# Attention values as float32 products on two column halves of TensorE, without a split of the exponentials

## The chip, the core and the metric

The kernel runs on one core of a Trainium2 chip, in one launch. The metric is the device time of that launch in microseconds (us). The engines of the core work side by side from their own queues, in the order in which the program lists their instructions: TensorE (PE in the profile; PEld is its loading of stationary operands), VectorE (DVE), ScalarE (ACT), GpSimd (POOL) and SyncE (SP), which issues most of the DMA transfers.

## The reference, cut to what matters

One layer of a diffusion backbone works on 128 context tokens and 1024 latent tokens: a modulated norm, one input projection, two branches (multi-head attention, and an mLSTM in two directions), a merge, an output projection and a feed-forward part. The change touches the attention alone. It has 8 heads, 96 numbers for a query or key and 64 for a value:

```
s = einsum('bqhd,bkhd->bhqk', qn_b, k_nope) + einsum('bqhr,bkr->bhqk', qp_b, k_pe)
p = softmax(s.astype(float32) * MLA_SCALE, axis=-1)
out = einsum('bhqk,bkhv->bqhv', p, v)
```

A context token attends to the 128 context keys. A latent token attends to 1152 keys: 1024 latent ones and 128 from a cache. All data are float32.

## The kernel before, in words

Most products in this kernel are made with a faster number format of TensorE, float32r, that keeps fewer bits. So each operand is first split in two parts: a leading part (`hi`, line 69, a copy on ACT) and the rest (`lo`, line 75, a subtraction on DVE). `mm3` (lines 95 to 100) then adds three products of such parts. Plain float32 products are used too: in the mLSTM (lines 1079 to 1084) and for sums over partitions (line 1449, for one).

The attention (`attention`, line 1183) goes through 40 units of work. Eight heads have five units each: four with 256 latent queries and nine blocks of 128 keys, and one with the 128 context queries and one block. A latent unit has five steps, of two key blocks each and one in the last. `scores` makes the scores of a step transposed, keys on the partitions, in the PSUM tile `st`; ACT takes their exponentials into `p` (line 1403). Then `p` is split: `ph` on ACT, `pl` on DVE (steps 0, 1 and 3) or on POOL (steps 2 and 4, line 1407). POOL adds up the exponentials in `es` (lines 1418 to 1422). Two steps later `values` multiplies `ph` and `pl` of each block by `v`, a stationary operand of 128 columns: 64 with the leading parts of the values, 64 with the rest (lines 1437 and 1438). All products of a unit add up in one PSUM tile `pv`.

`output` ends a unit in three pieces: the sums of the exponentials for each query, by float32 products with a column of ones (line 1449); their reciprocals, split into `rh` and `rl` and written on the diagonals of `dr` by ACT (line 1459); two products of 64 columns that spread them over 64 partitions (line 1462). Then the two halves of `pv` are added (line 1466), multiplied by the reciprocals (line 1467), split and stored to `d_att`.

Three things run beside it. `maxima` takes, one unit ahead, the greatest score of each query: products `mx` (line 1372), a DVE reduction of each (line 1374, `sm`), and a product that turns the result into a row (line 1382). `o_mlstm` multiplies the mLSTM output `hm` by its projection (tile `mm`, 384 columns). `head_load` and `head_split` fetch and split the next head's queries, keys and values, one piece a step. The instructions are recorded in one order and then placed on each engine by a scheduler that simulates a timeline; the engines follow that order and wait with semaphores.

Of the kernel before, what the change touches and what calls it, by code (L numbers as in the profile page):

```python
# [10 lines left out]
F32 = mybir.dt.float32  # L11
R32 = mybir.dt.float32r
# [7 lines left out]
P = 128  # L20
# [17 lines left out]
AV = 64  # L38
# [14 lines left out]
def f32v(ap):  # L53
    return ap.bitcast(F32)


class K:
# [25 lines left out]
    def load_w(self, src, kt, w, bufs=None):  # L83
        """Stream one weight block [P, kt, w] from DRAM and split it exactly."""
# [27 lines left out]
    def rsqrt(self, ssq, width, n, pool):  # L112
        """1/sqrt(ssq/n + eps) on the vector engine: exponent estimate and three Newton steps."""
# [12 lines left out]
    def row_rstd(self, rbc, acc, n, pool, pp, tag, chunks=CHUNKS, more=None):  # L126
        """rbc[:, t] = 1/sqrt(sum_p (acc[p, t] + more[p, t])/n + eps) on every partition."""
# [30 lines left out]
    def modulate(self, raw, t, sc, sh, k):  # L158
        """raw = t * sc + sh with the context's and the sample's own columns."""
# [4 lines left out]
    # ------------------------------------------------------------------  # L164
# [74 lines left out]
    def tick(self, n=1):  # L239
        """Emit n pieces of the work that runs beside the products."""  # L240
# [7 lines left out]
    def store(self, *args):  # L248
        """A store that is issued later, so that the loads behind it need not wait for its data."""
        self.stores.append(args)  # L250
# [8 lines left out]
    def rows(self, rbc, acc, n, pool, pp, tag):  # L259
        """rbc[:, t] = 1/sqrt(sum_p acc[p, t]/n + eps) on every partition."""  # L260
# [28 lines left out]
    def inputs(self):  # L289
        """Everything that reads the modulated input (all of w_in), the mLSTM and the attention's projections."""  # L290
# [38 lines left out]
    def start(self, vp):  # L329
        """Norm and modulation of the input, and the mLSTM's values."""  # L330
# [44 lines left out]
        def row(f):  # L375
            """Shift (f even) or scale of block 6 + f // 2 of the features, as rows against the broadcast condition."""
# [166 lines left out]
    def t_ops(self, X, xp):  # L543
        """The four sums on the moving side."""
# [29 lines left out]
    def z_lat(self, x):  # L574
        """Latents and their norms, and the tile with gates and rotary key."""
# [40 lines left out]
    def z_qk(self, h, x):  # L616
        """q and k of one mLSTM head, S^T and k^T."""
# [29 lines left out]
    def z_big(self, p, x):  # L647
        """sigmoid(zmo) * g_mlstm for tiles 0-7, the sigmoids of the branch gates after them."""
# [17 lines left out]
    def background(self):  # L666
        """Columns of the modulation that are used after the mixer, as rows against the broadcast condition."""
# [41 lines left out]
    def krope(self):  # L709
        """Rotary keys, 288 tokens to a row."""  # L710
# [16 lines left out]
    def gates(self):  # L727
        """Every per-token scalar of the two scans; row 64 d + 9 h + c holds chunk c of head h in direction d,
        whose scans run along the row, backwards for d = 1."""
# [66 lines left out]
        # N = -M, A = log of the denominator's floor  # L796
# [24 lines left out]
    def lat_kv(self):  # L821
        """The key and value latent, back from DRAM and split."""
# [19 lines left out]
    def stage(self):  # L842
        """Half a slot for a projected block."""
# [11 lines left out]
    def proj(self):  # L855
        """Keys, values and queries of the attention from the latents."""
# [94 lines left out]
    def fill(self, n=1):  # L951
        """Emit n column chunks of the attention's projections."""
# [5 lines left out]
    # ------------------------------------------------------------------  # L958
# [80 lines left out]
    def mfront(self, d, c, carried, second, S, E, Q, W):  # L1039
        """Operands of one chunk of one direction, four heads."""  # L1040
# [20 lines left out]
    def mback(self, d, c, carried, second, A, Q, K, C, mp, pp, side, load):  # L1061
        """Products, state update and output of the chunk."""
# [46 lines left out]
    def mpost(self, c, out, ssq, sgs, mp, pp):  # L1109
        """Norm, output gate and transposition of a finished chunk."""  # L1110
# [22 lines left out]
    # ------------------------------------------------------------------  # L1133
    def operands(self, pool):
        """Queries, keys and values of one head in two parts; row 96 adds -max of a query to its scores."""
        q = pool.tile([QK + 1, 2, T], R32, name=self.nm("q"))
        k = pool.tile([QK + 1, 2, NK], R32, name=self.nm("k"))
        v = pool.tile([P, NCH + 1, P], R32, name=self.nm("v"))
# [4 lines left out]
    def head_load(self, h, pool=None):  # L1143
        """Queries, keys (context, latent, cache) and values of one head, as column blocks."""
        G = self.nc.sync
        v = self.wp.tile([P, NCH + 1, AV], F32, name=self.nm("rv"), tag="wr", bufs=self.wb[0])
# [18 lines left out]
        G.dma_start(v, self.d_vo[h])  # L1165
        return q, k, v

    def head_split(self, h, raw):
        q, k, v = self.sets[h % 2]
        rq, rk, rv = raw  # L1170
# [5 lines left out]
        self.hi(v[:, :, 0:AV], rv)  # L1176
        self.lo(v[:, :, AV:], rv, v[:, :, 0:AV])
        yield 1

    SLOTS = 5  # L1180
    LAG = 2

    def attention(self):
# [6 lines left out]
        with tc.tile_pool(name="at", bufs=1, reuse_waits="tile") as ap:  # L1190
            self.ap, self.pp = ap, pp
            first = lambda shape, tag, bufs, dt=R32: ap.tile(shape, dt, name=self.nm(tag), tag=tag, bufs=bufs)
            for tag in ("ph", "pl"):
                first([P, 2, 256], tag, 4)
            first([P, 2, 256], "es", 2, F32)
            first([P, 2, 2, P], "dr", 1)
# [3 lines left out]
            self.onr = ap.tile([P, AV], R32, name="onr")  # L1200
            self.hi(self.onr, self.ones[:, 0:AV])
# [74 lines left out]
    def first(self):  # L1276
        """The first three products of two tiles of features, which don't wait for the last heads."""
# [15 lines left out]
    def early(self):  # L1293
        """The outputs of the first heads, in place of the operands of the last even one."""
# [9 lines left out]
    def fload(self, f, g, t):  # L1304
        """The gate of the attention's branch and the other branch."""
# [746 lines left out]
```

## Time and profile before

| | |
|---|---|
| time, median of 3 runs (lowest, highest) | 2248.58 us (2246.25, 2249.5) |
| span of the profiled execution, first to last instruction | 2242.8 us |
| the profiled execution's own time around the span | not given apart from the span; the median lies 5.8 us above it |
| PE busy, share of the span | 2083.1 us, 93% |
| DVE | 1659.5 us, 74% |
| ACT | 1068.0 us, 48% |
| POOL | 1127.2 us, 50% |
| granted TensorE clock, mean | 0.966 of full speed |
| attention, from its first product `mx` (848 us) to the last of `pv` (1263 us) | 415 us |

Busy time of PE counts an instruction until its modelled end, and a product begins before the one ahead of it has ended, so that a busy PE may still be waiting between starts. How much of the stage is really streamed is seen from the starts of successive products, or from their number and the distance between them.

### The profile page before, as it was taken

The numbers are of one execution on the slowest core, as the hardware profiler recorded it, in microseconds if no ns is written. First come the engines' busy times: TensorE is split into PE (matmuls) and PEld (weight loads), VectorE is DVE, ScalarE is ACT, GpSimd is POOL, SyncE is SP. The second block draws the span as 40 slices with busy tenths as digits, with TensorE's granted clock in tenths as the row PEclk, the third lists the DMA queues.
The fourth block names the chain that finished last, engine by engine and source line by source line (L and its number), as shares of the span: only waits on it lengthen the run. The fifth ranks groups of instructions, "written<-read, shape, count | busy, mean of one in ns | idle before, by whom it ended". The sixth has DMA issues, their size and how long they took to land.

```text
span 2242.8 us, 40186 instructions
## 1 busy us (share of the span) xinstructions
PE 2083.1 (93%) x14713; PEld 1998.2 (89%) x14713; DVE 1659.5 (74%) x2998; ACT 1068.0 (48%) x2225; POOL 1127.2 (50%) x850
## 2 busy tenths in 40 slices
PE   6799999999989987999999999879999999989898
PEld 2799998999978776998998999879999999989897
DVE  6725745988845879998987666899755565799895
ACT  4322333445445556777776435444322222356464
POOL 3612122667624415877877543677867634431411
PEclk8899999999999998999999999999999999999899
DMA  7121244555479775322224575223555522557664
GB/s 286 63 93 59 90 142 124 164 174 183 152 241 330 238 230 175 90 74 65 84 66 102 170 224 157 86 83 122 186 177 183 175 89 80 161 173 248 206 201 138
DMA packets 234532, 340.97 MB, mean 152 GB/s; under 512 B 18110, under 2 KB 170398, under 8 KB 233310
## 3 DMA queue, kind: packets, MB, share of 16 engines
q1 hardware_dynamic: 225790, 328.73, 46.0%
q0 software_dynamic: 4848, 6.06, 1.1%
q10 hardware_dynamic: 3696, 3.61, 0.5%
q8 instruction: 116, 1.90, 0.4%
q14 instruction: 82, 0.67, 0.1%
HBM read 250.55 MB, written 87.80 MB: 151 GB/s over the span
## 4 chain that ended last, share of the span: by engine, by line
PE 42%; DVE 16%; DMA 7%; POOL 6%; issue 6%; ACT 2%; SPq 1%; DVEq 0%; POOLq 0%; ACTq 0%
PE mm L98 10%; PE mm L100 10%; PE mm L99 10%; DVE wo L75 4%; DMA pr<-w_fo 3%; DVE sm L1374 2%; DVE pl L75 1%; PE st L98 1%; PE pv L1437 1%; PE pv L1438 1%; PE st L100 1%; PE st L99 1%; PE mx L1372 1%; DMA N<-d_nm 1%; PE p L1079 1%
## 5 line engine op out<-in xcount | busy, mean ns | idle before, releaser
L100 PE MATMUL mm<-th,wo 128*128 128x288 f32 x1840 | 546.8, 298 | 14.0 <-DVE wo L75 13.7
L98 PE MATMUL mm<-th,wo 128*128 128x288 f32 x1840 | 547.6, 298 | 2.7 <-DVE zo L1658 1.1
L99 PE MATMUL mm<-tl,wo 128*128 128x288 f32 x1840 | 546.2, 297 | 0.0
L100 PEld LDWEIGHTS mm<-th,wo 128*128 128x128 f32 x1840 | 348.9, 190 | 18.2 <-DVE wo L75 17.6
L75 DVE TENSOR_TENSOR wo<-wr,wo 128x512 fp32r<-128x512 f32 (+1 forms) x317 | 314.6, 1008 | 59.4 <-ACT wo L69 54.4
L98 PEld LDWEIGHTS mm<-th,wo 128*128 128x128 f32 x1840 | 348.2, 189 | 4.5 <-issue 1.6
L99 PEld LDWEIGHTS mm<-tl,wo 128*128 128x128 f32 x1840 | 348.3, 189 | 0.1
L69 ACT ACTIVATE wo<-wr 128x512 fp32r<-128x512 f32 (+1 forms) x317 | 187.5, 607 | 147.9 <-PE mm L100 69.5
L69 ACT ACTIVATE wo<-ws 128x512 fp32r<-128x512 f32 x188 | 116.7, 627 | 271.7 <-PE mm L100 160.5
L75 DVE TENSOR_TENSOR wo<-ws,wo 128x512 fp32r<-128x512 f32 x188 | 186.7, 996 | 62.1 <-ACT wo L69 61.9
L100 PE MATMUL mm<-xh,wo 128*128 128x288 f32 x616 | 184.7, 301 | 10.3 <-DVE wo L75 10.3
L1642 POOL TENSOR_TENSOR ws<-wr,ws 128x512 f32<-128x512 f32 x47 | 62.3, 1326 | 243.5 <-DVE wo L75 238.2
L99 PE MATMUL mm<-xl,wo 128*128 128x288 f32 x616 | 184.7, 300 | 0.0
L98 PE MATMUL mm<-xh,wo 128*128 128x288 f32 x616 | 184.2, 299 | 0.5 <-ACT wo L69 0.5
L1420 POOL TENSOR_TENSOR es<-es,p 128x512 f32<-128x512 f32 (+1 forms) x96 | 129.4, 1348 | 34.8 <-ACT p L1403 19.9
L98 PE MATMUL mm<-B,wo 128*128 128x288 f32 x456 | 134.8, 296 | 2.6 <-DVE zo L1658 1.7
L100 PE MATMUL mm<-B,wo 128*128 128x288 f32 x456 | 134.8, 296 | 0.0
L99 PE MATMUL mm<-B,wo 128*128 128x288 f32 x456 | 134.8, 296 | 0.0
L701 POOL TENSOR_TENSOR wm<-wm,sr 128x512 f32<-128x512 f32 x64 | 100.1, 1567 | 65.2 <-DVE mj L700 49.2
L100 PEld LDWEIGHTS mm<-xh,wo 128*128 128x128 f32 x616 | 118.1, 192 | 12.7 <-DVE wo L75 12.5
L98 PEld LDWEIGHTS mm<-xh,wo 128*128 128x128 f32 x616 | 118.2, 192 | 0.7 <-ACT wo L69 0.7
L99 PEld LDWEIGHTS mm<-xl,wo 128*128 128x128 f32 x616 | 118.4, 192 | 0.0
(443 smaller groups left out, 6076.6 us busy)
## 6 DMA issues: line engine op xcount, KB each, us to landing
wr<-w_ff SPq DMA_DIRECT2D x56, 512.0 KB
wm<-wm SPq DMA_DIRECT2D x32, 512.0 KB
wr<-d_w SPq DMA_DIRECT2D x32, 512.0 KB
d_z<-zo SPq DMA_DIRECT2D x48, 288.0 KB
d_g<-uu SPq DMA_DIRECT2D x44, 288.0 KB
wr<-w_big SPq DMA_DIRECT2D x24, 512.0 KB
wr<-w_fo SPq DMA_DIRECT2D x24, 512.0 KB
pr<-w_fo SPq DMA_DIRECT2D x40, 256.0 KB
```

The source lines that it names most:

```text
L69: i = self.nc.scalar.activation(out, in_, AF.Copy)
L75: return self.nc.vector.tensor_sub(out, in_, f32v(hi)).ins
L98: mm(out, lhs[0], rhs[0], start=first, stop=False)
L99: mm(out, lhs[0], rhs[1], start=False, stop=False)
L100: self.pe = mm(out, lhs[1], rhs[0], start=False, stop=last).ins
L701: nc.gpsimd.tensor_tensor(w[:, n], w[:, n], sr[:, 1], op=ALU.mult)
L1079: self.pe = mm(p1, A[:, h], V[:, h], start=True, stop=not carried).ins
L1372: nc.tensor.matmul(s[:, :kc], q[0:QK, 0, q0 + t * P:q0 + (t + 1) * P], k[0:QK, 0, k0 + j * kc:k0 + (j + 1) * kc], start=True, stop=True)
L1374: nc.vector.tensor_reduce(sm[:, 3 * t + j:3 * t + j + 1], s[:, :kc], axis=AX.X, op=ALU.max, negate=True)
L1420: G.tensor_tensor(U["sum"][:, :m], U["sum"][:, :m], p[:, :m], op=ALU.add)
L1437: nc.tensor.matmul(pv[:, :n], v[:, i], ph[:, e, :n], start=c + e == 0, stop=False)
L1642: G.tensor_tensor(s4, a12, s2, op=ALU.subtract)
```

## The change

The exponentials are not split any more, and neither are the values. `p` has six buffers of its own and goes into the products as float32, with `v` as 64 float32 columns. The two key blocks of a step are multiplied one after the other in the program, the first on columns 0 to 63 of TensorE (partitions 0 to 63 of `pv`), the second on columns 64 to 127. The last block, which has no partner, is cut in two halves of the queries that go the same way. The sums of the exponentials are made by one float32 product with a stationary operand of ones, 64 columns wide, which leaves the sum of each query on all 64 partitions; DVE then takes the reciprocal of a tile of 64x256 and multiplies by it. The values of the next head are fetched straight into their place, at the beginning of `head_split` in place of the end of `head_load`. Comments are taken out as well, which moves line numbers.

```diff
 def operands(self, pool):
-        v = pool.tile([P, NCH + 1, P], R32, name=self.nm("v"))
+        v = pool.tile([P, NCH + 1, AV], F32, name=self.nm("v"))
...
 def head_load(self, h, pool=None):
-        v = self.wp.tile([P, NCH + 1, AV], F32, name=self.nm("rv"), tag="wr", bufs=self.wb[0])
...
-        G.dma_start(v, self.d_vo[h])
-        return q, k, v
+        return q, k
 def head_split(self, h, raw):
         q, k, v = self.sets[h % 2]
-        rq, rk, rv = raw
+        rq, rk = raw
+        self.nc.sync.dma_start(v, self.d_vo[h])
...
-        self.hi(v[:, :, 0:AV], rv)
-        self.lo(v[:, :, AV:], rv, v[:, :, 0:AV])
-        yield 1
...
+    PBUF = 6
...
 def scores(self, U, c):
-        p = self.wp.tile([P, 2, 256], F32, name=self.nm("p"), tag="ws", bufs=3)
+        p = ap.tile([P, 2, 256], F32, name=self.nm("p"), tag="p", bufs=self.PBUF)
         self.ia = nc.scalar.activation(p[:, :m, :n], st[:, :m, :n], AF.Exp).ins
-        ph, pl = (ap.tile([P, 2, 256], R32, name=self.nm(x), tag=x, bufs=4) for x in ("ph", "pl"))
-        self.hi(ph[:, :m, :n], p[:, :m, :n])
-        if c in (2, 4):
-            nc.gpsimd.tensor_tensor(pl[:, :m, :n], p[:, :m, :n], f32v(ph[:, :m, :n]), op=ALU.subtract)
-        else:
-            self.iv = self.lo(pl[:, :m, :n], p[:, :m, :n], ph[:, :m, :n])
-        U["P"][c] = ph, pl
+        U["P"][c] = p
...
 def values(self, U, c):
-        ph, pl = U["P"].pop(c)
-        for e, i in enumerate(kb[2 * c:2 * c + 2]):
-            nc.tensor.matmul(pv[:, :n], v[:, i], ph[:, e, :n], start=c + e == 0, stop=False)
-            self.pe = nc.tensor.matmul(pv[:, :n], v[:, i], pl[:, e, :n], start=False, stop=i == kb[-1]).ins
+        p = U["P"].pop(c)
+        blocks = kb[2 * c:2 * c + 2]
+        if len(blocks) == 2:
+            parts = [(i, e, 0, n) for e, i in enumerate(blocks)]
+        else:
+            parts = [(blocks[0], 0, t * n // 2, n // 2) for t in range(2)]
+        for g, (i, e, q0, w) in enumerate(parts):
+            self.pe = nc.tensor.matmul(pv[g * AV:(g + 1) * AV, q0:q0 + w], v[:, i], p[:, e, q0:q0 + w], start=c == 0,
+                                       stop=c == U["nc"] - 1, skip_group_check=True).ins
...
 def output(self, U):
-        for t in range(nt):
-            nc.tensor.matmul(pv[:, 256 + t:257 + t], U["sum"][:, 0, t * P:(t + 1) * P], self.ones[:, 0:1], start=True, stop=True)
-        rd = ap.tile([P, 2], F32, name=self.nm("rd"), tag="rd", bufs=2)
-        nc.vector.reciprocal(rd[:, :nt], pv[:, 256:256 + nt])
...
-        for t in range(nt):
-            for e, x in enumerate((f32v(rh), rl)):
-                nc.scalar.activation(dg[:, e, t], self.ident, AF.Copy, scale=x[:, t:t + 1])
+        nc.tensor.matmul(pv[0:AV, 256:256 + n], self.ones[:, 0:AV], U["sum"][:, 0, :n], start=True, stop=True, skip_group_check=True)
         yield 1
-        for e in range(2):
-            nc.tensor.matmul(pv[0:AV, 256:256 + n], self.onr[:, 0:AV], dg[:, e, :nt].rearrange("p t q -> p (t q)"),
-                             start=e == 0, stop=e == 1)
...
+        rd = ap.tile([AV, 256], F32, name=self.nm("rd"), tag="rd", bufs=2)
+        nc.vector.reciprocal(rd[:, :n], pv[0:AV, 256:256 + n])
+        nc.vector.tensor_mul(t2[:, :n], t2[:, :n], rd[:, :n])
```

On TensorE before, in the second head: the end of a unit (`onr` by `dr`) and the first step of the next, whose two key blocks take four products.

```order
L1462 MATMUL pv_10018<-dr_10101,onr 64x128 x2
L1382 MATMUL mx_10265<-selr,mr_10154 1x256
L1437 MATMUL pv_10064<-ph_9973,v_9240 128x256
L1438 MATMUL pv_10064<-pl_9974,v_9240 128x256
L1437 MATMUL pv_10064<-ph_9973,v_9240 128x256
L1438 MATMUL pv_10064<-pl_9974,v_9240 128x256
L98 MATMUL mm_9987<-hm_9373,wh_9757 128x384
```

On TensorE now, in the same head: two steps of a unit. `x2` stands for two products of one form, here those of the two key blocks.

```order
L1429 MATMUL pv_9876<-p_9835,v_9235 64x256 x2
L1365 MATMUL mx_9863<-k_9234,q_9233 128x384
L98 MATMUL st_9903<-q_9233,k_9234 128x256
L99 MATMUL st_9903<-q_9233,k_9234 128x256
L100 MATMUL st_9903<-q_9233,k_9234 128x256
L1429 MATMUL pv_9876<-p_9857,v_9235 64x256 x2
L98 MATMUL mm_9819<-hm_9397,wh_9641 128x384
L99 MATMUL mm_9819<-hm_9397,wh_9641 128x384
```

The four products of a step have become two of half the width, one behind the other, with products of full width on both sides.

On DVE before, between two reductions of the maxima: the split of exponentials, and reciprocals with their split.

```order
L75 TENSOR_TENSOR pl_9806<-p_9803,ph_9805 128x512
L1467 TENSOR_TENSOR av_9727<-av_9727,pv_9522 64x256
L1377 TENSOR_REDUCE mr_9912<-sm_9911 128x1
L1451 RECIPROCAL rd_9840<-pv_9682 128x2
L1455 CAST rh_9843<-rd_9840 128x2
L1374 TENSOR_REDUCE sm_9911<-mx_9923 128x1
L75 TENSOR_TENSOR rl_9844<-rd_9840,rh_9843 128x2
```

On DVE now, at the end of a unit of the second head.

```order
L1445 TENSOR_TENSOR av_10029<-av_10029,pv_9876 64x256
L1450 RECIPROCAL rd_10032<-pv_9876 64x256
L1367 TENSOR_REDUCE sm_9938<-mx_9991 128x1
L1367 TENSOR_REDUCE sm_9938<-mx_9994 128x1
L75 TENSOR_TENSOR q_6949<-rq_9787,q_6949 96x576
L75 TENSOR_TENSOR q_6949<-rq_9790,q_6949 96x576
L1451 TENSOR_TENSOR av_10029<-av_10029,rd_10032 64x256
```

The subtractions `pl` and `rl` and the cast `rh` are gone from between the reductions, and a reciprocal of 256 columns stands there.

## Rows read from the trace of the kernel before

**Rows 1.** The page: the span, and the busy time of each engine.

```profile
span 2242.8 us, 40186 instructions
PE 2083.1 (93%) x14713; PEld 1998.2 (89%) x14713; DVE 1659.5 (74%) x2998; ACT 1068.0 (48%) x2225; POOL 1127.2 (50%) x850
```

**Rows 2.** Busy time by stretch: the whole attention, two stretches within it at full clock and one at a lower clock. The last three columns are the granted clock, the DMA share and GB/s.

```profile
848.00:1263.00 415.00, 384.38 (x2583) 360.69 (x2582) 361.91 (x698) 291.00 (x659) 302.41 (x241) 0.95 0.32 90
...
950.00:1000.00 50.00, 48.66 (x343) 46.03 (x343) 47.01 (x94) 36.50 (x87) 40.14 (x30) 1.00 0.26 74
...
1050.00:1100.00 50.00, 48.10 (x351) 46.72 (x350) 46.04 (x93) 37.28 (x88) 40.15 (x32) 1.00 0.25 73
1150.00:1200.00 50.00, 47.35 (x309) 45.27 (x309) 41.94 (x90) 34.17 (x79) 37.30 (x33) 0.90 0.22 59
```

**Rows 3.** The groups of products on PE between 848 and 1263 us: line, tiles, rows x columns of the stationary and of the moving operand, number, busy time and mean ns of one, idle time before them. A float32 product has two records, so that line 1449 shows 128 for 64.

```profile
L98 PE MATMUL st<-q,k 97*128 97x256 f32 x288 | 86.1, 299 | 1.5 <-ACT p L1403 0.9 <-ACT q L1383 0.4
...
L1437 PE MATMUL pv<-ph,v 128*128 128x256 f32 x288 | 81.8, 299 | 5.7 <-DVE av L1467 5.7
L1438 PE MATMUL pv<-pl,v 128*128 128x256 f32 x288 | 80.8, 301 | 3.2 <-DVE pl L75 1.7 <-POOL pl L1407 1.4
L1372 PE MATMUL mx<-k,q 96*128 96x384 f32 x192 | 65.2, 375 | 10.6 <-DVE sm L1374 9.8
L98 PE MATMUL mm<-hm,wh 128*128 128x384 f32 x184 | 64.2, 349 | 0.6 <-DVE t L1354 0.6
...
L1382 PE MATMUL mx<-selr,mr 128*1 128x256 f32 x72 | 20.0, 289 | 8.3 <-DVE mr L1377 4.0 <-DVE mr L1379 3.7 <-DVE sm L1374 0.4
L1462 PE MATMUL pv<-dr,onr 128*64 128x256 f32 x64 | 17.7, 284 | 0.1
L1449 PE MATMUL pv<-ones,es 128*128 128x1 f32 x128 | 16.3, 230 | 0.3 <-POOL es L1422 0.3
```

**Rows 4.** PE in order of time at full clock, in the attention: start, duration, line and tiles. The first five show a product of 64 columns between products of 128, the last two the four records of two float32 sums and the start behind them.

```profile
1000.19 0.34 PE L99 MATMUL mm<-hm,wh 128*128 128x384 f32 x1
1000.37 0.34 PE L100 MATMUL mm<-hm,wl 128*128 128x384 f32 x1
1000.54 0.28 PE L1462 MATMUL pv<-dr,onr 128*64 128x256 f32 x1
1000.66 0.28 PE L1437 MATMUL pv<-ph,v 128*128 128x256 f32 x1
1000.77 0.34 PE L1372 MATMUL mx<-k,q 96*128 96x384 f32 x1
...
1001.82 0.61 PE L1449 MATMUL pv<-ones,es 128*128 128x1 f32 x4 [0.35 <-POOL es L1422]
1002.28 0.42 PE L1372 MATMUL mx<-k,q 96*128 96x384 f32 x1
```

**Rows 5.** PE in order of time in the mLSTM: float32 products of 257 columns, each with its two records.

```profile
702.62 0.60 PE L1079 MATMUL p<-V,N 128*128 128x257 f32 x2
703.06 0.59 PE L1081 MATMUL p<-C,Q 128*128 128x257 f32 x2
703.49 0.60 PE L1079 MATMUL p<-V,N 128*128 128x257 f32 x2
```

**Rows 6.** PE in order of time at 1216 us, in a stretch of half clock.

```profile
1216.60 0.41 PE L99 MATMUL st<-q,k 97*128 97x256 f32 x1
1216.81 0.41 PE L100 MATMUL st<-q,k 97*128 97x256 f32 x1
1217.02 0.41 PE L98 MATMUL st<-q,k 97*128 97x256 f32 x1
```

**Rows 7.** Who waited for whom between 848 and 1263 us: the total in us, how often, the longest. Two waits of PE for the maxima, one of its weight loads for a split, and one of ACT for PE.

```profile
ACT p L1403 <- PE st L100: 35.7, 33, 3.9
...
PEld mx L1372 <- DVE sm L1374: 17.6, 29, 2.3
...
PE mx L1372 <- DVE sm L1374: 10.0, 13, 2.0
...
PEld pv L1438 <- DVE pl L75: 3.8, 9, 1.0
```

**Rows 8.** The groups on DVE, ACT and POOL between 848 and 1263 us that the change removes or alters: busy time, mean ns, idle before.

```profile
L75 DVE TENSOR_TENSOR pl<-p,ph 128x512 fp32r<-128x512 f32 x96 | 88.5, 924 | 20.9 <-ACT ph L69 18.7 <-issue 1.9
...
L75 DVE TENSOR_TENSOR rl<-rd,rh 128x2 f32<-128x2 f32 x32 | 22.1, 691 | 0.3
...
L1455 DVE CAST rh<-rd 128x2 fp32r<-128x2 f32 x32 | 15.7, 490 | 0.3
...
L1466 DVE TENSOR_TENSOR av<-av,pv 64x256 f32<-64x256 f32 x31 | 12.5, 402 | 0.2 <-ACT av L1465 0.2
...
L1451 DVE RECIPROCAL rd<-pv 128x2 f32<-128x2 f32 x32 | 5.0, 157 | 3.8 <-PE pv L1449 3.8
...
L1451 DVE RECIPROCAL rd<-pv 128x1 f32<-128x1 f32 x8 | 1.2, 151 | 0.0
...
L69 ACT ACTIVATE ph<-p 128x512 fp32r<-128x512 f32 x128 | 79.0, 626 | 3.5 <-PE pv L1437 1.3 <-PE pv L1438 1.0
...
L1407 POOL TENSOR_TENSOR pl<-p,ph 128x512 fp32r<-128x512 f32 x32 | 48.7, 1522 | 2.1 <-ACT ph L69 2.1
L1407 POOL TENSOR_TENSOR pl<-p,ph 128x256 fp32r<-128x256 f32 x32 | 36.2, 1132 | 9.1 <-ACT ph L69 9.1
```

More of the change, by code (lines that the diff above doesn't have):

```diff
@@ L1192, in attention @@
             first = lambda shape, tag, bufs, dt=R32: ap.tile(shape, dt, name=self.nm(tag), tag=tag, bufs=bufs)
-            for tag in ("ph", "pl"):
-                first([P, 2, 256], tag, 4)
+            first([P, 2, 256], "p", self.PBUF, F32)
             first([P, 2, 256], "es", 2, F32)
-            first([P, 2, 2, P], "dr", 1)
             first([AV, 256], "av", 2, F32)
@@ L1199, in attention @@
             self.sets.append(self.operands(ap))
-            self.onr = ap.tile([P, AV], R32, name="onr")
-            self.hi(self.onr, self.ones[:, 0:AV])
             self.sel = ap.tile([P, 3 * P], R32, name="selr")
@@ L1373, in maxima @@
                                  start=True, stop=True)
-                nc.vector.tensor_reduce(sm[:, 3 * t + j:3 * t + j + 1], s[:, :kc], axis=AX.X, op=ALU.max, negate=True)
+                self.iv = nc.vector.tensor_reduce(sm[:, 3 * t + j:3 * t + j + 1], s[:, :kc], axis=AX.X, op=ALU.max, negate=True).ins
                 yield
@@ L1445, in output @@
         h, n, pv = U["h"], U["n"], U["pv"]
-        nt = n // P
         yield 1
-        for t in range(nt):
-            nc.tensor.matmul(pv[:, 256 + t:257 + t], U["sum"][:, 0, t * P:(t + 1) * P], self.ones[:, 0:1], start=True, stop=True)
-        rd = ap.tile([P, 2], F32, name=self.nm("rd"), tag="rd", bufs=2)
-        nc.vector.reciprocal(rd[:, :nt], pv[:, 256:256 + nt])
-        dg = ap.tile([P, 2, 2, P], R32, name=self.nm("dr"), tag="dr", bufs=1)
-        rh = ap.tile([P, 2], R32, name=self.nm("rh"), tag="rh", bufs=2)
-        rl = ap.tile([P, 2], F32, name=self.nm("rl"), tag="rl", bufs=2)
-        nc.vector.tensor_copy(rh[:, :nt], rd[:, :nt])
-        self.lo(rl[:, :nt], rd[:, :nt], rh[:, :nt])
-        for t in range(nt):
-            for e, x in enumerate((f32v(rh), rl)):
-                nc.scalar.activation(dg[:, e, t], self.ident, AF.Copy, scale=x[:, t:t + 1])
+        nc.tensor.matmul(pv[0:AV, 256:256 + n], self.ones[:, 0:AV], U["sum"][:, 0, :n], start=True, stop=True, skip_group_check=True)
         yield 1
-        for e in range(2):
-            nc.tensor.matmul(pv[0:AV, 256:256 + n], self.onr[:, 0:AV], dg[:, e, :nt].rearrange("p t q -> p (t q)"),
-                             start=e == 0, stop=e == 1)
         t2 = ap.tile([AV, 256], F32, name=self.nm("av"), tag="av", bufs=2)
-        nc.scalar.copy(t2[:, :n], pv[AV:, :n])
-        nc.vector.tensor_add(t2[:, :n], t2[:, :n], pv[0:AV, :n])
-        nc.vector.tensor_mul(t2[:, :n], t2[:, :n], pv[0:AV, 256:256 + n])
+        if U["nc"] > 1:
+            nc.scalar.copy(t2[:, :n], pv[AV:, :n])
+            nc.vector.tensor_add(t2[:, :n], t2[:, :n], pv[0:AV, :n])
+        else:
+            nc.scalar.copy(t2[:, :n // 2], pv[0:AV, :n // 2])
+            nc.scalar.copy(t2[:, n // 2:n], pv[AV:, n // 2:n])
+        rd = ap.tile([AV, 256], F32, name=self.nm("rd"), tag="rd", bufs=2)
+        nc.vector.reciprocal(rd[:, :n], pv[0:AV, 256:256 + n])
+        nc.vector.tensor_mul(t2[:, :n], t2[:, :n], rd[:, :n])
         at = ap.tile([AV, 2, 256], R32, name=self.nm("ao"), tag="ao", bufs=2)
```

## The prediction

> **What bounds the kernel now.** I read the page first: PE is busy for 93% of the span and DVE for 74% [rows 1], so the question is which of them holds the attention, the only stage that the change touches. The busy time by stretch answers for the stage [rows 2]: in 415 us PE is busy for 384 and DVE for 362, in the stretches at full clock 48.7 and 48.1 of 50 for PE and 47.0 and 46.0 for DVE. The two stand nearly level. The groups on PE [rows 3] and the starts of neighbours [rows 4] tell how much of PE's time is streaming. At full clock a float32r product of 256 columns starts 0.12 us before its successor and one of 384 columns 0.17 to 0.18; a record of a float32 sum takes 0.46/4 = 0.115. Rows 3 hold 3 x 288 scores, 2 x 288 values, 72 rows of maxima and 64 spreads, 1576 products of 256 columns: 189 us. The 192 products `mx` and 3 x 184 products `mm` of 384 columns make 130 us, the 128 records of sums 15. That is 334 us; small groups that rows 3 leave out add some 10. So about 70 of 415 us are not streamed.
>
> Two things fill these 70 us. The mean granted clock is 0.95 [rows 2], and at half clock the starts lie 0.21 apart in place of 0.12 [rows 6]: 5% of 415 is 21 us lost to the lower of the two levels, 1.2 in place of 2.4 GHz. The rest, some 49 us, is waiting. The waits [rows 7] name DVE most: PE and its weight loads wait 10.0 and 17.6 us for the reductions `sm` of the maxima, which stand in DVE's queue behind splits (the order of DVE shows them in turn), and a weight load waits 3.8 us for `pl`. ACT waits 35.7 us for scores, so it is not what holds the stage.
>
> **The change part by part.** The price on PE, for one unit of 256 queries:
> - Removed: 18 value products at 0.12, 2.16 us; four records of sums at 0.115, 0.46; two spreads at 0.12, 0.24. Together 2.86 us.
> - Added, the sum product: one float32 product of 256 columns. The float32 products of the mLSTM, of 257 columns, start 0.43 to 0.44 us apart, and each has two records [rows 5]: 0.216 a record, 0.43 for the product.
> - Added, the values: four steps of two float32 products of 256 columns, and one of two of 128. No row of before shows two products on different column halves, so this cost is bounded. If the halves share no time, a step is four records, 0.86. If they share all of it, 0.43. The order puts the two products of a step one behind the other, and a product's own two records need the same columns; if starts keep to the order, only the second record of the first product can run beside the first record of the second. That is three records, 0.65 us, and 0.32 for the last step. I take this middle: 4 x 0.65 + 0.32 = 2.92.
>
> The unit then costs 3.35 us, 0.49 more than before; 32 units make +16 us on PE. With no sharing it is 4 x 0.86 + 0.43 + 0.43 = 4.30, +1.44 a unit, +46 us; with full sharing 4 x 0.43 + 0.22 + 0.43 = 2.37, -0.49 a unit, -16 us. The eight context units have a few short products on either side and are put at nothing; with 0.1 us each they would be 1 us.
>
> The Trainium skill (TensorE: Matmul & The Clock Gate, Part 3, The mechanism) states that products on different column tiles run at the same time and that products start strictly in order; by that a step would be the three records. No run here shows it yet.
>
> The price elsewhere [rows 8]: DVE loses `pl` (88.5 us), `rl` (22.1), `rh` (15.7) and the short reciprocals (5.0 and 1.2), 132 us. It gains 32 reciprocals of 64x256. Before shows none of that size. Below, it costs what an addition of that shape does, 0.40 us. Above, the step from one column to two took 6 ns (151 to 157), and 254 more such steps make 0.16 + 1.52 = 1.7 us. I take the upper value, since it comes from the same operation: 54 us, where the lower would be 13. DVE then stands at 362 - 132 + 54 = 284 us, 68% of the stage in place of 87%. ACT loses 79 us of `ph` and all diagonals, POOL 48.7 + 36.2 = 85 us. All three fall below PE, which alone bounds the stage.
>
> What comes back of the 70 us: in the two stretches at full clock PE is idle for 1.3 and 1.9 us of 50, 3.2%, and in the whole stage for 31 of 415, 7.4% [rows 2]. If the stage ran throughout as these stretches do, 31 would shrink to 13, and the 21 us of the clock would return: 39 us. With DVE relieved I take that, 40 us, although the cause of some waits (the next head's operands, the end of a unit) stays. Bounds: nothing returns (DVE's waits only change their name, since the reciprocal now stands in front of reductions), or 63 of 70.
>
> Two parts are put at nothing. Fetching the values moves on SP's queue from behind the next head's keys to the beginning of its split, and now waits for PE's last reading of the head that used the place; behind it stand loads for `mm` and stores of `d_att`. The reader is about a unit older by then (a unit is 415/40 = 10 us). If the cover were gone, 1 us at each of seven heads would be 7 us. And the chain at a unit's end loses the diagonals but gains the long reciprocal, and has a unit's time to spare, since `pv` has two buffers. The order of the mLSTM stage shifts a little, which I put at 0 with 2 us to either side.
>
> The sum: +16 - 40 = -24 us on a span of 2242.8, 2219; the median of the runs lies 5.8 us above that span, so **2225 us**.
>
> **The rivals.**
> 1. The halves share no time, so that the change does not do what it says: +46 - 40 = +6, 2255 us; with the bounds of the return from 2232 to 2295. For it: nothing in the trace shows two products at a time. Against: nothing shows that they cannot.
> 2. The halves share all their time: -16 - 40 = -56, 2193 us. For it: the products of a step are neighbours. Against: the two records of one product [rows 5] come in succession, so the fourth is left over.
> 3. Slower: each change between full and half width empties the array first. The price is the part of a product that otherwise overlaps the next start: it lasts 0.28 us and the next starts after 0.12 [rows 4], so 0.16 us a change. A unit has five steps and a sum, 12 changes, of which about 10 are left where two follow each other: 32 x 10 x 0.16 = 51 us, on top of the forecast +27, 2276 us. It decides from 24 us on, 0.075 us a change. Against it: the spread of 64 columns stands between products of 128 and starts 0.17 us after a product of 384 columns, its successor 0.12 us later [rows 4], as if nothing changed.
>
> The Trainium skill (TensorEngine Tiling (Array Packing), Key Properties) states that changing the tiling mode drains TensorE, which is rival 3. By that rule a price like the 51 us is due; by rows 4 it is zero at the first column half, and for the second no row speaks.
>
> **How the numbers follow.** Chances: forecast 0.40, rival 1 0.28, rival 2 0.17, rival 3 0.15. A difference under 0.2%, 4.5 us, counts as none here, about what a measurement of this kernel can tell. The forecast's own range is its bounds of the return, +16 - 63 and +16 - 0: 2202 to 2265; I give it 0.33 faster, 0.03 same, 0.04 slower. Rival 1 lies across zero: 0.07, 0.07, 0.14. Rival 2 is faster, 0.17; rival 3 is slower but for 0.01. Together 0.57 faster, 0.11 same, 0.32 slower. The range from 2195 to 2275 leaves out half of rivals 2 and 3 and the far end of rival 1.
>
> **What would show it.** In the starts of PE, the step of two products: 0.65 us from the first record to the full-width product behind it (rival 1 0.86, rival 2 0.43), and no extra gap at either side (rival 3). In the groups on DVE, a reciprocal of 64x256 near 1.7 us and DVE under 70% of the stage. In the waits, PE for `sm` well below 27 us, and a granted clock nearer to 1. The attention, 415 us before, about 391. The forecast is wrong if PE's waits keep their sum under other names, or if other stages move by more than 5 us.

## The result, and the profile after

The changed kernel takes 2256.58 us (median of 13 runs) where the kernel before takes 2247.78 (13 runs on the same chip): a ratio of 1.004, 95% interval 1.0026 to 1.0054, so 9 us slower. One of its runs, at 7168 us, stands far outside all others and is left out of the ratio. The forecast was 2225.

The page of the profiled execution gives the span and the busy times, to be read beside [rows 1].

```profile
span 2252.7 us, 39320 instructions
PE 2107.2 (94%) x14649; PEld 1941.1 (86%) x14649; DVE 1593.1 (71%) x2798; ACT 939.6 (42%) x1912; POOL 1034.5 (46%) x786
```

DVE lost 66 us and POOL 93, as the change meant; PE gained 24. The busy time by stretch, the whole attention and three stretches, answers to [rows 2]:

```profile
849.00:1265.00 416.00, 401.25 (x2477) 296.83 (x2477) 292.69 (x499) 164.03 (x349) 212.41 (x178) 0.96 0.32 89
950.00:1000.00 50.00, 49.71 (x325) 36.68 (x323) 36.23 (x62) 20.17 (x44) 25.95 (x21) 1.00 0.25 69
1050.00:1100.00 50.00, 49.50 (x320) 36.49 (x318) 37.26 (x62) 20.02 (x43) 26.53 (x22) 1.00 0.28 74
1150.00:1200.00 50.00, 48.36 (x309) 37.72 (x309) 34.66 (x60) 19.22 (x42) 25.06 (x20) 0.97 0.22 60
```

DVE has fallen from 87% of the stage to 70%, and PE now stands still for 0.3 and 0.5 us of 50 at full clock, where it was 1.3 and 1.9. By these rows hardly anything keeps PE waiting there, yet it is no sooner done: its own work has become longer. Who waited for whom, beside [rows 7]:

```profile
ACT p L1396 <- PE st L100: 115.3, 105, 4.0
...
PEld pv L1440 <- POOL es L1409: 10.5, 7, 4.7
...
PE pv L1440 <- POOL es L1409: 8.6, 7, 4.5
...
PEld mx L1365 <- DVE sm L1367: 8.1, 20, 0.9
...
PE mx L1365 <- DVE sm L1367: 1.4, 3, 0.7
```

The two waits for `sm` fell from 27.6 us to 9.5. ACT waits three times as long for PE, which costs nothing, since ACT isn't the bound. One wait is new: the sum product of a unit (line 1440) stood 8.6 us behind POOL's addition of the sums, in seven places; in the kernel before, the sums hardly waited (0.3 us, [rows 3]).

Where PE's time goes is seen in its starts, in order of time at full clock:

```profile
999.63 0.65 PE L1429 MATMUL pv<-p,v 128*64 128x256 f32 x4
1000.21 0.44 PE L1365 MATMUL mx<-k,q 96*128 96x384 f32 x1
1000.49 0.29 PE L98 MATMUL st<-q,k 97*128 97x256 f32 x1
1000.62 0.28 PE L99 MATMUL st<-q,k 97*128 97x256 f32 x1
1000.74 0.28 PE L100 MATMUL st<-q,k 97*128 97x256 f32 x1
1000.95 0.65 PE L1429 MATMUL pv<-p,v 128*64 128x256 f32 x4
1001.53 0.45 PE L100 MATMUL mm<-hm,wl 128*128 128x384 f32 x1
1001.81 0.34 PE L98 MATMUL mm<-hm,wh 128*128 128x384 f32 x1
1001.99 0.34 PE L99 MATMUL mm<-hm,wh 128*128 128x384 f32 x1
```

The step of two halves is the second row with x4 (1000.95), its four records. The scores product ahead of it starts 0.21 us earlier (1000.74 to 1000.95), where its successor would follow after 0.12. The product behind the step starts 0.58 us later (1000.95 to 1001.53), and its own successor after 0.28 (1001.53 to 1001.81), where 0.18 is usual for 384 columns. If the four records take 0.43 us, as two records in succession do, then 0.09 before, 0.15 within and 0.10 behind are left over: 0.34 us for each stay of PE at half width. I call such a stay, a run of half-width float32 products between other products, a group. In the order of the changed kernel there are 177 of them; 177 x 0.34 = 60 us.

On DVE the new reciprocal, in the groups of that engine, beside the ones of 128x2 and 128x1 in [rows 8]:

```profile
L1450 DVE RECIPROCAL rd<-pv 64x256 f32<-64x256 f32 x32 | 55.8, 1743 | 0.0
...
L1450 DVE RECIPROCAL rd<-pv 64x128 f32<-64x128 f32 x8 | 7.2, 899 | 0.0
```

### The profile page after: what moved, and what is told of

Its sections match the earlier page's. It is cut to its first block, busy times and chain, and to the rows that moved or that the text cites. A ratio compares the mean times of both kernels' runs of the same rounds, so it can differ in the third digit from the quotient of the medians.

```text
span 2252.7 us, 39320 instructions
## 1 busy us (share of the span) xinstructions
PE 2107.2 (94%) x14649; PEld 1941.1 (86%) x14649; DVE 1593.1 (71%) x2798; ACT 939.6 (42%) x1912; POOL 1034.5 (46%) x786
## 3 DMA queue, kind: packets, MB, share of 16 engines
q8 instruction: 115, 1.88, 0.3%
## 5 line engine op out<-in xcount | busy, mean ns | idle before, releaser
L1367 DVE TENSOR_REDUCE sm<-mx 128x1 f32<-128x384 f32 (+1 forms) x200 | 101.2, 532 | 72.5 <-PE mx L1365 71.6
L1396 ACT ACTIVATE p<-st 128x512 f32<-128x512 f32 (+2 forms) x168 | 90.4, 539 | 123.8 <-PE st L100 115.3
L100 PEld LDWEIGHTS mm<-xh,wo 128*128 128x128 f32 x616 | 117.4, 191 | 12.0 <-DVE wo L75 11.8
```

What stands on the lines that cost most here:

```text
L1367: self.iv = nc.vector.tensor_reduce(sm[:, 3 * t + j:3 * t + j + 1], s[:, :kc], axis=AX.X, op=ALU.max, negate=True).ins
L1396: self.ia = nc.scalar.activation(p[:, :m, :n], st[:, :m, :n], AF.Exp).ins
```

## The experiments

The theory after this reading: the halves share all their time, and each group costs 0.34 us because PE changes its width. Rivals: the price lies in float32 records as such, in the end of a unit (reciprocal, sum), or in waits.

**1. Widths by themselves.** A small kernel with products alone; the layer is left out. It ran once; the sections stand at full clock (1.00 granted from 20 to 72 us). Its sections repeat two full-width float32r products (`xr`, line 36) and a piece of half-width ones (line 39), float32 (`xf`) or float32r: `fpair` has one product on each half, `fone` one product on one half, `fthree` three pairs, `rone` one float32r product on the lower half; `ffpair` sets a pair behind one full-width float32 product; `fburst` has pairs alone, with full-width products behind the eighth.

> This kernel leaves out the whole layer and fills its outputs with constants: on TensorE it runs rows of products alone, in sections named by their PSUM tile, each of eight rounds of two float32r products of full width and a piece. Theory (a change of width costs TensorE some 0.35 us for each group of half-width float32 products, and the two halves share all their time): a round of fpair (piece: the two halves) takes 2 x 0.12 + 0.43 + 0.35 = 1.02 us, fone (one half) as much, 1.02; rone (piece: a float32r product of 64 columns) 0.36, without any price; ffpair (one float32 product of full width, then the two halves) 1.21; fthree (three pairs as piece) 1.88; fburst (pairs alone) 0.43 a pair. Rival (the halves share nothing and a change of width is free): fpair 1.10, fone 0.67, ffpair 1.29, fthree 2.83, fburst 0.86.

PE in order of time in these sections:

```profile
21.16 0.50 PE L36 MATMUL fpair<-xr 128*128 128x256 f32 x2
21.59 0.65 PE L39 MATMUL fpair<-xf 128*64 128x256 f32 x4
22.17 0.50 PE L36 MATMUL fpair<-xr 128*128 128x256 f32 x2
...
29.26 0.50 PE L36 MATMUL fone<-xr 128*128 128x256 f32 x2
29.69 0.65 PE L39 MATMUL fone<-xf 128*64 128x256 f32 x2
30.26 0.50 PE L36 MATMUL fone<-xr 128*128 128x256 f32 x2
...
36.76 0.40 PE L36 MATMUL rone<-xr 128*128 128x256 f32 x2
36.99 0.28 PE L39 MATMUL rone<-xr 128*64 128x256 f32 x1
37.10 0.40 PE L36 MATMUL rone<-xr 128*128 128x256 f32 x2
...
39.73 0.65 PE L39 MATMUL ffpair<-xf 128*64 128x256 f32 x4
40.31 0.70 PE L36 MATMUL ffpair<-xf 128*128 128x256 f32 x2
40.94 0.65 PE L39 MATMUL ffpair<-xf 128*64 128x256 f32 x4
...
48.80 0.51 PE L36 MATMUL fthree<-xr 128*128 128x256 f32 x2
49.23 1.52 PE L39 MATMUL fthree<-xf 128*64 128x256 f32 x12
50.68 0.50 PE L36 MATMUL fthree<-xr 128*128 128x256 f32 x2
...
63.71 3.62 PE L39 MATMUL fburst<-xf 128*64 128x256 f32 x32
67.27 0.50 PE L36 MATMUL fburst<-xr 128*128 128x256 f32 x2
```

A round of `fpair` takes 1.01 us (21.16 to 22.17), one of `fone` 1.00 (29.26 to 30.26): the second half is free, so sharing is full. Two full products at 0.12 and two records at 0.216 make 0.67; 0.34 is left over. A round of `fthree` takes 1.88 us (48.80 to 50.68), and 0.24 + 6 x 0.216 = 1.54: again 0.34, so the price is for a group, whatever its length. In `ffpair` the full product is float32 too, and a round of 1.21 us against 4 x 0.216 = 0.86 leaves 0.35: the neighbour's format doesn't matter. In `rone` three products take 0.34 us (36.76 to 37.10), 0.115 each: a float32r product of 64 columns, the one form that [rows 4] show, costs nothing. Eight pairs of `fburst` take 3.56 us to the full product behind them (63.71 to 67.27), which is 8 x 0.43 and the 0.09 of the one change at their end: without products of full width between them the pairs pay nothing, and 0.43 a pair is full sharing.

The weight loads of the same sections show something more:

```profile
21.15 0.30 PEld L36 LDWEIGHTS fpair<-xr 128*128 128x128 f32 x2 [0.39 <-issue]
21.59 0.20 PEld L39 LDWEIGHTS fpair<-xf 128*64 128x64 f32 x4
22.17 0.30 PEld L36 LDWEIGHTS fpair<-xr 128*128 128x128 f32 x2 [0.38 <-issue]
...
36.88 0.14 PEld L39 LDWEIGHTS rone<-xr 128*64 128x64 f32 x1
```

In `rone` the weights of the narrow product are loaded 0.11 us before it starts (36.88 and 36.99), beside the product ahead of it. In `fpair` the first load on either side of a change starts together with its product (21.15 and 21.16, 21.59 and 21.59); ahead of the full-width one PEld stands still for 0.39 us, and the profile shows nothing that it waits for. So at a change the next product's weights are not loaded ahead. How much of the price is this and how much the products themselves, no run parts. The same is seen in the changed kernel, where the load behind the step starts at 1001.53 like its product.

**2. All value products on one half.**

```diff
-        for g, (i, e, q0, w) in enumerate(parts):
-            self.pe = nc.tensor.matmul(pv[g * AV:(g + 1) * AV, q0:q0 + w], v[:, i], p[:, e, q0:q0 + w], ...
+        for e, i in enumerate(blocks):
+            self.pe = nc.tensor.matmul(pv[0:AV, :n], v[:, i], p[:, e, :n], ...
...
```

> The changed kernel with all key blocks on columns 0 to 63, so that nothing can be shared; the changes of width stay (182 groups), the addition of the two halves falls away. Theory (halves share all their time): a step costs two records of 0.216 us more and the last one as much more, 32 x 4 x 0.43 + 32 x 0.22 = +62 us, 2318 us (2300 to 2330). Rival 1 (halves share nothing): 2256, unchanged within 6. Rival 2: between, nearer to unchanged, because the end of a unit gets shorter: 2245 to 2285.

Measured: 2309.12 us against 2243.55, ratio 1.0294 (1.027 to 1.0318), 66 us slower than before and some 57 above the changed kernel. 62 was expected: without sharing each step costs two more records, and 32 x (4 x 0.43 + 0.22) = 62. In the kernel, too, sharing is full.

**3. The same at full width.** The weights of each value product become two neighbouring key blocks, 128 columns, of which one's 64 result rows are used; the sum product gets 128 columns of ones. The number of float32 records stays as in 2, and no half width is left.

```diff
-            self.pe = nc.tensor.matmul(pv[0:AV, :n], v[:, i], p[:, e, :n], ...
+            j = max(i - 1, 0)
+            self.pe = nc.tensor.matmul(pv[:, :n], v[:, j:j + 2].rearrange("p i d -> p (i d)"), p[:, e, :n], ...
...
-        nc.tensor.matmul(pv[0:AV, 256:256 + n], self.ones[:, 0:AV], U["sum"][:, 0, :n], ...
+        nc.tensor.matmul(pv[:, 256:256 + n], self.ones, U["sum"][:, 0, :n], ...
...
```

> As the run with all value products on one half, with the same number of float32 records in the same free order, but each product is full width: its 128 weight columns are two neighbouring key blocks, of which one's 64 result rows are used and the other's are ignored; the sum is full width too. No half-width float32 product is left, so no group. By 0.34 us a group, 182 x 0.34 = 62 us less than the run on one half, which was 66 us slower than before: 4 us slower than before, and 5 us faster than the changed kernel. If the price lies in float32 records as such, in their order or in the waits, and not in the width, it is as slow as the run on one half (66 us slower than before).

Measured: 2255.7 us against 2246.53, ratio 1.0049 (1.003 to 1.0068): 9 us slower than before (4 was expected), where the half-width twin is 66 us slower. 56 us for 182 groups is 0.31 us each. Its starts in order of time:

```profile
1002.90 0.28 PE L1375 MATMUL mx<-selr,mr 128*1 128x256 f32 x1
1003.02 1.03 PE L1426 MATMUL pv<-p,v 128*128 128x256 f32 x4
1003.70 0.52 PE L98 MATMUL mm<-hm,wh 128*128 128x384 f32 x1
1004.05 0.34 PE L99 MATMUL mm<-hm,wh 128*128 128x384 f32 x1
```

The float32 products begin 0.12 us after the row product ahead, without the gap of the halves. Behind them there is none either: the first product of `mm` is recorded early, at 1003.70, but from 1003.02 to its second one it takes 1.03 us, and four records and one product of 384 columns are 4 x 0.216 + 0.17 = 1.03. So it isn't the float32 records as such, and not the waits: with the same records at full width the price is gone. Since the float32r product of experiment 1 doesn't pay either, it takes both, float32 and half width. The kernel is as fast as the changed one, with no halves at all: what sharing saves (62 us), the changes of width take (60).

**4. The old sums.** The end of a unit as before (columns of ones, short reciprocals, diagonals, two spreads), the values as changed.

```diff
-        nc.tensor.matmul(pv[0:AV, 256:256 + n], self.ones[:, 0:AV], U["sum"][:, 0, :n], ...
+        for t in range(nt):
+            nc.tensor.matmul(pv[:, 256 + t:257 + t], U["sum"][:, 0, t * P:(t + 1) * P], self.ones[:, 0:1], ...
...
+            nc.tensor.matmul(pv[0:AV, 256:256 + n], self.onr[:, 0:AV], dg[:, e, :nt].rearrange("p t q -> p (t q)"), ...
...
```

> The changed kernel with the sums of before: columns of ones, short reciprocals, diagonals, two float32r products of 64 columns. Groups of half-width float32 products fall from 177 to 160. Theory: 17 groups x 0.35 = -6 us, and about the same work on TensorE: 2250 us (2243 to 2256). Rival 2 (the reciprocal of 1.74 us on DVE and the sum product behind POOL hold the stage): the loss goes and more, 2215 to 2238.

Measured: 2253.1 us against 2243.55, ratio 1.0045 (1.0028 to 1.0062), as slow as the changed kernel. So the long reciprocal and the new sum together are not what the change lost. The run doesn't price them one by one: the new sum's wait for POOL goes (waits over 1 us fall from 10 to 3 us in the table below) and 17 groups with it, but the four short records and two spreads take 0.27 us a unit more on PE than the new sum product, 9 us.

**5. A full-width sum, values as changed.** Only the last line of the diff in 3.

> The product that spreads the sums writes all 128 rows (128 columns of ones) instead of 64, so that it is a full-width float32 product. As built, the groups of half-width products that stand between full-width ones fall from 177 to 156. If each such group costs 0.34 us (the bare measurement), 21 x 0.34 = 7 us come back: about 2 us slower than before. If the price lies in something else than the change of width (the float32 records, the waits), the time stays at 9 us slower than before.

Measured: 2248.69 us against 2247.37, ratio 1.001 (0.9993 to 1.0027): 1.3 us slower where 2 was expected. A product twice as wide as it needs to be gave back nearly all that the change had lost. Not all of it need be the groups: in the table below 5 us lie in the rest, near the 7 for 21 groups, and 6 in a clock that stood at half for 19 us in place of 31, which this run does not explain.

**6. Values held back, fewer groups.** In the next runs the order of PE is tied: at a batch of value products, all that was recorded earlier runs before it and all that was recorded later behind it. First a whole unit with its sum as one batch.

```diff
+    def burst(self, late, m):
+        self.inb = True
+        for _ in range(m):
+            self.values(*late.pop(0))
+        self.inb, self.wall = False, self.seen[-1]
...
-                    while len(late) > self.LAG:
-                        self.values(*late.pop(0))
+                    m = late[0][0]["nc"]
+                    if len(late) >= m + self.LAG:
+                        self.burst(late, m)
```

> The changed kernel, with the value products of a unit and its sum product made in one go, two steps after the unit's last scores, and eight buffers of p. The groups of half-width products fall from 177 to 42. Theory (0.35 us for each group): 135 groups less, -47 us, 2210 us (2200 to 2222). Rival 1 (no sharing, change of width free): 2256, unchanged within 5. Rival 2 (the end of a unit holds the stage: the sum product waits for POOL, the long reciprocal delays the maxima): 2256 to 2275, since the sum product now stands in front of everything behind the burst.

Measured: 2331.0 us against 2243.55, ratio 1.0378 (1.0355 to 1.0401): a miss, 87 us slower than before. To part the ties from the number of groups, the next three (with the full-width sum of 5) have batches of one, two and three steps, `burst(late, 1)`, `2` and `3`; `p` has 6, 8 and 9 buffers. With three, a batch also waits for one step of scores behind it and not for two (`LAG`).

> The same, and the order of TensorE's products in attention is tied at each step: all that was written before a step's two halves runs before them, all behind them after. 168 groups. This is the control for the next two: it has the ties without fewer groups. If ties cost nothing, 6 us slower than before. If ties as such are what made the run with a burst for each unit slow (it stood 75 us above the changed kernel with 42 groups), this one is 30 us or more slower than before.

> The same ties, but the halves of two steps stand together: 85 groups. By 0.34 us a group it is 83 x 0.34 = 28 us faster than the run with 168 tied groups, whatever the ties cost; with free ties 22 us faster than before. If the number of groups is not what costs, it is as slow as the run with 168 tied groups.

> Three steps together, 59 groups. By 0.34 us a group 37 us below the run with 168 tied groups. The rival for this one: value products are what TensorE does while the chain of a unit's maximum (VectorE's reductions, the row, ScalarE's copy) is under way; the longer they are held together, the longer TensorE stands before that chain's products, so this one is no faster than the run with two steps together, and its idle time before the maximum's products is larger.

Measured against 2247.37: one step 2296.74, ratio 1.0224 (1.0186 to 1.0262); two 2303.08, 1.025 (1.0217 to 1.0283); three 2266.15, 1.0093 (1.0062 to 1.0124). Against experiment 5 one tied step is 48 us slower, of which 12 more groups explain 4: the ties alone cost some 44. Two steps together brought nothing where 28 us were expected, three brought 31 of 37 and are faster than two, which the rival in their expectation excluded; what their earlier start did can't be told apart from their length. Of the run with two steps, PE in order of time:

```profile
1002.00 0.28 PE L1186 MATMUL mx<-selr,mr 128*1 128x256 f32 x1
1005.11 0.28 PE L1186 MATMUL mx<-selr,mr 128*1 128x256 f32 x1 [2.83 <-DVE mr L1402]
1005.32 1.08 PE L1186 MATMUL pv<-p,v 128*64 128x256 f32 x8
```

The row product of the maxima waits 2.83 us for DVE, and the values that could have run meanwhile are tied behind it. The attention by stretch, of the runs with one step, two, three and a whole unit, in that order:

```profile
849.00:1265.00 416.00, 389.17 (x2195) 288.34 (x2194) 260.27 (x460) 152.46 (x316) 167.01 (x157) 0.90 0.29 81
```

```profile
849.00:1265.00 416.00, 362.91 (x2211) 288.33 (x2210) 259.22 (x461) 153.03 (x321) 167.39 (x156) 0.90 0.28 78
```

```profile
849.00:1265.00 416.00, 373.14 (x2399) 307.21 (x2397) 284.35 (x494) 162.57 (x343) 187.48 (x171) 0.93 0.30 85
```

```profile
849.00:1265.00 416.00, 351.71 (x2075) 277.69 (x2076) 241.95 (x435) 141.16 (x299) 166.38 (x139) 0.87 0.26 74
```

The granted clock fell to 0.87 to 0.93, where the changed kernel had 0.96. The table below takes waits and clock apart from the rest. The stretch runs from the first scores to the first product of the merge; its time at half clock (half of which is lost) and its waits (starts over 1 us apart, less 0.2) are added up from the starts and the clock in the traces, and "rest" is the stretch without that half and without the waits. Each row is one profiled execution, which lies up to 8 us from the median of its runs.

| kernel | groups | stretch | at half clock | waits | rest |
|---|---|---|---|---|---|
| before | 0 | 459.9 | 41.0 | 24.5 | 414.9 |
| changed | 177 | 466.8 | 30.7 | 10.4 | 441.0 |
| one half (2) | 182 | 517.9 | 18.2 | 6.4 | 502.4 |
| all wide (3) | 0 | 466.1 | 18.3 | 12.3 | 444.7 |
| old sums (4) | 160 | 465.6 | 23.9 | 3.4 | 450.2 |
| full-width sum (5) | 156 | 456.8 | 18.7 | 11.2 | 436.2 |
| tied, one step | 168 | 513.5 | 88.0 | 19.2 | 450.3 |
| tied, two steps | 85 | 517.3 | 94.7 | 48.2 | 421.7 |
| tied, three steps | 59 | 477.9 | 57.3 | 31.1 | 418.1 |
| tied, a unit | 42 | 541.2 | 123.9 | 52.9 | 426.3 |
| three steps, maxima free (7) | 70 | 454.8 | 20.5 | 19.7 | 424.9 |
| also side products free (7) | 72 | 457.1 | 32.3 | 15.9 | 425.0 |
| the same, two steps (7) | 95 | 470.6 | 39.2 | 26.6 | 424.4 |

From one step to two the rest falls by 28.6 us for 83 groups, 0.34 each, as expected; in the time it can't be seen, because the waits grew by 29. From experiment 2 to experiment 3 it falls by 58 for 182 groups. The column isn't clean, since waits under 1 us stay in it: tied at one step it is 14 us above experiment 5, of which 12 more groups explain 4.

**7. Ties without the maxima.** As with three steps, but the products of the maxima are left free and may stand anywhere, and a batch waits for two steps of scores again; then the products of `o_mlstm` are free too; then the latter with two steps.

```diff
 def maxima(self, h, b):
-                nc.tensor.matmul(s[:, :kc], ...
+                self.mm0(s[:, :kc], ...
...
-            nc.tensor.matmul(r[0:1, 0:256], ...
+            self.mm0(r[0:1, 0:256], ...
```

> As the run with three steps together, but the products of the maximum's chain are not tied (they may stand before, behind or between), and the halves wait one step longer: 70 groups. Stretch from the first scores of attention to the first gate product of the merge: with 156 untied groups it took 456.8 us, 10.2 of them lost to half clock and 11.2 in waits over 1 us. If the ties' price was TensorE standing before the maximum's products, and the clock falling with it, both stay near those 21 us, and 86 groups fewer by 0.34 us give 29 us: stretch 428 us, 28 us faster than before. If the ties of scores and values are enough to make TensorE wait (60 us as with all tied), stretch 466 us, 8 us slower than before.

> Also the products of the mLSTM's output, which run beside attention, are free of ties: 72 groups. By 0.34 us a group alone 28 us off the run with 156 groups, 27 us faster than before. If it is clearly below the run in which only the maximum's products are free, the ties of the side products cost time of their own; if equal, the maximum's products were what counted.

> The same with two steps together: 95 groups. By 0.34 us a group 21 us off the run with 156 groups, 20 us faster than before, 8 us above the run with 72 groups. If it is faster than that, the length of a burst costs more in waits than the fewer groups bring.

Measured against 2246.45: maxima free 2242.05, ratio 0.9979 (0.9965 to 0.9993); side products free too 2245.42, 0.9997 (0.9984 to 1.001); with two steps 2257.32, 1.0052 (1.0034 to 1.007). The first is 4 us faster than the kernel before and the only run here that is faster than it beyond its interval. It got its clock back, by stretch 0.98:

```profile
849.00:1265.00 416.00, 388.67 (x2581) 320.53 (x2581) 282.83 (x503) 167.61 (x354) 203.61 (x178) 0.98 0.32 89
```

But 28 us were expected, and 27 and 20 of the other two. Against experiment 5 its rest fell by 11 us, not by 29. The pauses between full-width products under 1 us, beyond the usual distance of their forms, add up to 9 us at full clock in experiment 5 and to 25 here, which is nearly all that is missing. The waits that the profile names grew likewise: PE waits 15 us for the chain of the maxima, its row and its copy on ACT, where it was 3, and 10 us for the weights of `mm`, where it was 0.5. This fits the reading that the values, when they are not batched, are what PE does while a unit's maxima pass through DVE and ACT; no run shows it by itself. The two runs with free side products agree: two steps have 23 groups more than three and nearly the same rest, 424.4 and 425.0, because their short pauses are fewer (19 us for 28); their waits over 1 us are longer (26.6 us for 15.9). I did not settle which of scores, maxima and side products would have to move to keep the whole gain.

## Why the prediction was wrong

**The price of a change of width, put at nothing, is the step that failed.** Rival 3 named the right term and nearly the right size: 0.16 us a change from the overlap of [rows 4], 51 us; measured 0.34 us a group, that is 0.17 for each of its two changes, 60 us. It got a chance of 0.15 because the prediction argued against it from the spread of line 1462, a product of 64 columns without a gap. That product is float32r, and experiment 1 shows that this form has no price while the float32 form has. The rule of the Trainium skill (TensorEngine Tiling (Array Packing), Key Properties), that a change of tiling mode drains TensorE, agrees with the 0.34 us of the float32 halves and with the weight loads that start only with their product; that the array is empty meanwhile no row shows directly. It does not show in the float32r product on the lower half; whether that one changes the mode at all, no run tells.

**The step of three records was wrong too, to the other side.** The four records take the time of two. The starts in the trace are the first records of both halves 6 ns apart and the second ones together 0.27 us after the first: the second half does not wait until the first has sent both of its records. That is rival 2, so the values and the sum cost -16 us, not +16. The Trainium skill (TensorE: Matmul & The Clock Gate, Part 3, The mechanism) says that products on different column tiles run at the same time, which the trace confirms. The three records that the prediction drew from the strict order it does not. The sign it had named for them misleads: 0.65 us from the first record to the full-width product behind was forecast and 0.58 measured, but that is 0.43 of full sharing and 0.15 of the change of width.

**The waits that come back were right.** By the prediction's own count 334 - 16 + 10 = 328 us are streamed now and 60 go to the changes; 28 of 416 are left, where 70 of 415 were. Part of that was only moved: 15 products of `o_mlstm` and 30 of `att` by `wo` that the stage had held, 6 us by their distances, now stand behind it (the last part of `o_mlstm` starts at 1273.7 us where it was 1266.8). That makes 36 us returned, predicted 40. It is a remainder of this count, but the starts bear it out: from before to now, pauses under 1 us between full-width products at full clock fell from 27 us to 4, waits over 1 us from 24 to 10, and the half clock costs 5 us less, 42 together, without the pauses beside the groups. DVE came out at 293 us and 70% of the stage (284 and 68% predicted); 7 us of the difference are the eight reciprocals of the context units, which the sum had left out. The reciprocal took 1.74 us (1.7), the waits for `sm` fell to 9.5 us. The clock rose less than hoped, 0.95 to 0.96, and the sum product's new wait for POOL, 8.6 us, stood in no step of the prediction.

**The sum, mended:** -16 + 60 - 36 = +8 us on the span; the trace shows +10 (2242.8 to 2252.7), and the other 2 lie in other stages, within what was allowed. No value product waited for a DMA transfer, so the fetch of the values showed no cost. The forecast missed by 32 us, which is less than the failed step alone, because the step of three records erred by 32 us the other way: that is luck, not a nearly right sum.

So the true pieces were named but put together wrongly: the step of three records was the middle of its bounds, and the change of width was put at nothing by a row that had the shape and not the format of the new product. Rivals 2 and 3 don't exclude each other, and no case held both.

## What to carry to other kernels

Float32 products of 64 columns, set one by one among full-width ones, cost 0.34 us for each stay, here as much as the sharing of the halves saves (60 and 62 us). Widen those that share nothing (experiment 5), or set many together where nothing waits meanwhile; in this kernel the best such order gained 4 us. When a row is to show that a thing costs nothing, look whether it has the same number format, not the shape alone. And before products are gathered, ask what they were filling: from one tied step to two, half the groups fell away and the waits took back all that this saved, 29 us.

## What the runs showed that I had not expected

- The price is the same for one half-width product, a pair and three pairs (0.33, 0.34 and 0.34 us), and behind a full-width float32 product (0.35); the float32r product of 64 columns on the lower half has none, and neither have half-width pairs that follow each other.
- It lies in three places: 0.09 us before the first record, 0.15 within and up to the product behind, 0.10 behind that one.
- The reciprocal takes 6.6 ns a column: 899 ns for 128 and 1743 for 256, whereas additions of a tile of 64x256 take 407.
- A fully tied order, with PE waiting before the maxima, stood at half clock for 57 to 124 us of the stretch, all others for 18 to 41.
